# Seven products over the whole depth for the down projections of a hybrid decoder layer

## The chip, the cores and the metric

The kernel runs on one core of one Trainium2 chip. The metric is the device time of one execution in microseconds (us), as the median of several runs on the chip. One execution was also recorded by the hardware profiler; where a text speaks of a place in time, it is the time of that trace, counted from the start of its span.

## What is computed

One decoder layer on 1024 tokens of width 1024, all in float32: a feed-forward network (FFN), a mixer (a gated delta rule beside a Mamba-2 scan), a second FFN, a final RMS norm. The change touches the two FFNs alone, and in them the last product of `swiglu`:

```python
D_MODEL = 1024; SEQ = 1024; D_FF = 2816
def rms_norm(x, w):
    return x * lax.rsqrt(jnp.mean(x * x, axis=-1, keepdims=True) + EPS) * w
def swiglu(h, w_gate, w_up, w_down):
    a = jnp.einsum("bld,df->blf", h, w_gate)
    b = jnp.einsum("bld,df->blf", h, w_up)
    return jnp.einsum("blf,fd->bld", jax.nn.silu(a) * b, w_down)
...
        x = x + 0.5 * swiglu(rms_norm(x, ffn1_norm[i]), ffn1_w_gate[i], ffn1_w_up[i], ffn1_w_down[i])
        x = x + hybrid_mixer(rms_norm(x, mix_norm[i]), ...)
        x = x + 0.5 * swiglu(rms_norm(x, ffn2_norm[i]), ffn2_w_gate[i], ffn2_w_up[i], ffn2_w_down[i])
    return rms_norm(x, final_norm)
```

Below, *hid* is `silu(a) * b`, 1024 tokens by 2816; the down projection is hid times `w_down` (2816 by 1024).

## The kernel before

**Arithmetic.** TensorE works on fp32r data. A float32 operand is split in a high part (a cast, on ScalarE) and a low part (operand minus high part, on VectorE), and each product of two operands is three matmuls: high by high, high by low, low by high (`mm3`, L119 to L121; L311 to L313 in the gate and up phase). One matmul takes 128 of the depth by 128 tokens by 512 columns and adds into a PSUM bank of 128 x 512.

**Stages.** Normalise x and transpose it; gate and up of FFN 1 (`gate_up_all`); its down projection (`down_all`); the mixer; gate and up and down of FFN 2; the final norm. Gate and up already go by Strassen's seven products of 2 x 2 blocks, for 256 columns of hid at a time (pass `p`, 11 of them): the four 512-token quarters `s12, s21, s11, s22` of hid (two column blocks `j` by two token halves) come out of VectorE and are stored in a DRAM scratch, `hid_scr[n][p]` (L390, four stores of 256 KB).

**The down projection before.** `down_all` goes through the depth in 11 groups `g` of 256. For a group, `hid_load` (L401) fetches four pieces of 256 KB from the scratch and splits them, and `load_rows_w` (L152) fetches 1 MB of `w_down` and splits it (`wsplit`, L134 on ScalarE and L135 on VectorE). Then `tile_` is called for 8 token blocks `b` by 2 column halves `dh`: six matmuls into one PSUM bank, and one instruction that adds half of it to the running sum `xt[b]` (VectorE, L420; in group 0, ScalarE writes it, L418). The x of the residual is added piece by piece on the way (L443). The last two groups are taken together, twelve matmuls to a bank, so that a token block is finished as soon as its two banks are: `done(b)` then stores it to `x_scr` and, after blocks 5 and 7, normalises and transposes half of the tokens for the mixer (FFN 1, `norm_mix`), or makes the final norm of the block and stores its output (FFN 2, `finish`, L1209 to L1225). An FFN has 11 x 16 x 6 = 1056 such matmuls in its down projection. All loads and stores named here are issued by SyncE (SP) in program order; a load waits there until its buffer is free, and those behind it in the program wait with it. The order of the instructions on each engine is fixed when the kernel is built.

**Buffers.** `wst` (raw weights) has two buffers, `whi` and `wlo` (split weights) two each; `b0` to `b5` are six buffers in which the gate and up phase keeps operands, and the down projection the split hid. PSUM banks go by tags: `mx` and `sc` two each, `pj` three, `oo` one.

Of the kernel before, what the change touches and what calls it, by code (L numbers as in the profile page):

```python
# [31 lines left out]
NG = GH + SH  # L32
COL_Q, COL_K, COL_V, COL_GZ = 0, 1024, 2048, 3072
# [10 lines left out]
def kernel(  # L44
# [25 lines left out]
    hid_scr = [[dram.tile([P, 2, L], F32, name=f"hid_scr{n}_{i}") for i in range(NF2)] for n in range(2)]  # L70
# [231 lines left out]
    def gate_up_all(pool, H, w_gate, w_up, scr, raws, ops, work, tail):  # L302
# [25 lines left out]
        for i, (p, w) in enumerate(todo):  # L328
# [63 lines left out]
    def hid_load(pool, scr, g):  # L392

        th, tl = (("b0", "b1"), ("b2", "b3"))[g % 2]
        hh = hbp[0].tile([P, 2, L], F32R, name="hid_h", tag=th)
        hl = hbp[0].tile([P, 2, L], F32R, name="hid_l", tag=tl)
        for half in range(2):
            ts = slice(half * 512, (half + 1) * 512)
            for j in range(2):
                t = pool.tile([P, 512], F32, name="hd", tag="q")  # L400
                nc.sync.dma_start(out=t, in_=scr[g][:, j, ts])  # L401
                split(hh[:, j, ts], hl[:, j, ts], t)
        return hh, hl

    def down_all(pool, xt, x_src, w_down, scr, start, before_last, last_tags, done):
        cnt = [0]

        def tile_(tags, b, dh, parts, new=False):
            bs, ds = slice(b * P, (b + 1) * P), slice(dh * 512, (dh + 1) * 512)
            pd = psum(tags[cnt[0] % len(tags)])  # L410
            cnt[0] += 1
            n = 2 * len(parts)
            for i in range(n):
                (hh, hl), (wh, wl) = parts[i // 2]
                j = i % 2
                mm3(pd, hh[:, j, bs], hl[:, j, bs], wh[:, j, ds], wl[:, j, ds], i == 0, i == n - 1)
            if new:
                A.mul(out=xt[b][:, ds], in_=pd, mul=0.5)  # L418
                return
            V.scalar_tensor_tensor(out=xt[b][:, ds], in0=pd, scalar=0.5, in1=xt[b][:, ds],  # L420
                                   op0=ALU.mult, op1=ALU.add)

        nxt = start[0]
        for g in range(NF2 - 2):
            cur = nxt
            hid = hid_load(pool, scr, g + 1)
            if g + 1 < NF2 - 2:
                nxt = hid, load_rows_w(wp, w_down, (g + 1) * 256, "")
            else:
                st = wp.tile([P, 2, D], F32, name="wst", tag="wst")  # L430
                nc.sync.dma_start(out=st, in_=w_down[(g + 1) * 256:(g + 2) * 256].rearrange("(c p) d -> p c d", p=P))
                wh = hbp[0].tile([P, 2, D], F32R, name="whd", tag="b4")
                wl = hbp[0].tile([P, 2, D], F32R, name="wld", tag="b5")
                for j in range(2):
                    split(wh[:, j], wl[:, j], st[:, j])
                nxt = hid, (wh, wl)
            for b in range(NB):
                for dh in range(2):
                    if g == 3 + b // 2:
                        t = pool.tile([P, 512], F32, name="xin", tag="q")  # L440
                        nc.sync.dma_start(out=t, in_=x_src[:, b, dh * 512:(dh + 1) * 512])
                        o = xt[b][:, dh * 512:(dh + 1) * 512]
                        V.tensor_tensor(out=o, in0=o, in1=t, op=ALU.add)  # L443
                    tile_(("mx", "sc", "mx", "sc", "oo"), b, dh, [cur], g == 0)
        last = hid_load(pool, scr, NF2 - 1), load_rows_w(wp, w_down, (NF2 - 1) * 256, "")
        before_last()
        for b in range(NB):
            for dh in range(2):
                tile_(last_tags, b, dh, [nxt, last])
            done(b)  # L450
# [48 lines left out]
    def gate_up_phase(n, npool, H, w_gate, w_up, w_down, raws, ops):  # L499
        start = []  # L500

        def tail_hid():
            start.append([hid_load(npool, hid_scr[n], 0)])

        def tail_w():
            start[0].append(load_rows_w(wp, w_down, 0, ""))

        with tc.tile_pool(name=f"work{n}", bufs=1, side="right", reuse_waits="tile") as work:
            gate_up_all(npool, H, w_gate, w_up, hid_scr[n], raws, ops, work, [tail_hid, tail_w])
        return start  # L510


    with ExitStack() as c1:
# [18 lines left out]
        start = gate_up_phase(0, npool, H, ffn1_w_gate[0], ffn1_w_up[0], ffn1_w_down[0], raws, ops)  # L532
# [719 lines left out]
```

## Time and profile before

| | |
|---|---|
| median of 3 runs | 2404.14 us (2402.14 to 2407.81) |
| profiled execution | 2402.77 us, of which the span of the trace is 2401.1 us |
| TensorE (PE) busy | 2346.9 us, 98% of the span, 12062 matmuls |
| VectorE (DVE) busy | 1680.8 us, 70% |
| ScalarE (ACT) busy | 1042.5 us, 43% |
| DMA | 227.41 MB on SP's queue, packets taking 29.1% of 16 engines' span |
| down projection of FFN 1 | first matmul 462.19 us, last 708.65 us |
| down projection of FFN 2 | first matmul 2150.41 us, last 2391.24 us |

PE's busy time is the time in which matmuls are recorded as running; their ends are modelled, so it says that PE had work, not that it was at its peak. How fast PE goes is read from the distance of one matmul's start to the next.

### The profile page before, as it was taken

How to read it: one execution, taken by the hardware profiler on the slowest of the kernel's cores; microseconds unless marked ns; L12 is line 12 of the kernel's file. 1: busy time of each engine (PE TensorE's matmuls, PEld its weight loads, DVE VectorE, ACT ScalarE, POOL GpSimd, SP SyncE). 2: the span in 40 equal slices, each digit the busy share in tenths (PEclk: the TensorE clock that was granted, in tenths of full speed). 3: DMA queues.
4: the chain of work that ended last, by engine and by line, in shares of the span. 5: the costliest groups of instructions: out<-in, count | busy, mean ns of one | idle time of the engine just before them, and what ended most of it. 6: DMA issues, size and time to landing. Idle time of an engine off the chain costs nothing.

```text
span 2401.1 us, 32017 instructions
## 1 busy us (share of the span) xinstructions
PE 2346.9 (98%) x12062; PEld 1923.1 (80%) x12062; DVE 1680.8 (70%) x3393; ACT 1042.5 (43%) x1972; POOL 52.9 (2%) x117
## 2 busy tenths in 40 slices
PE   6999999999999999999999999999999999999998
PEld 4788888788887878788888888778778888888886
DVE  7766666567756664668777878778686666665777
ACT  7433333422146775863455555412543333343122
POOL 0000000000000010100000000000000000000000
PEclk9999999999999999999999999999999999999999
DMA  2222222433322321222222223235122222242432
GB/s 107 97 81 102 72 88 70 158 105 132 116 106 72 106 88 53 71 91 62 80 80 80 73 78 95 80 121 213 62 88 88 79 80 94 83 151 87 149 106 79
DMA packets 199850, 229.47 MB, mean 96 GB/s; under 512 B 45241, under 2 KB 151926, under 8 KB 198670
## 3 DMA queue, kind: packets, MB, share of 16 engines
q1 hardware_dynamic: 199694, 227.41, 29.1%
q8 instruction: 95, 1.56, 0.3%
q14 instruction: 61, 0.50, 0.1%
HBM read 176.95 MB, written 50.43 MB: 95 GB/s over the span
## 4 chain that ended last, share of the span: by engine, by line
PE 82%; DVE 6%; issue 5%; ACT 4%; DMA 2%; POOL 0%; SPq 0%; DVEq 0%; POOLq 0%; ACTq 0%
PE ps_pj L121 8%; PE ps_pj L119 8%; PE ps_pj L120 8%; PE ps_pj L312 6%; PE ps_pj L311 6%; PE ps_pj L313 6%; PE ps_mx L311 3%; PE ps_mx L312 3%; PE ps_mx L313 3%; PE ps_mx L119 3%; PE ps_mx L121 2%; PE ps_mx L120 2%; PE ps_sc L119 2%; PE ps_sc L121 2%; PE ps_sc L120 2%
## 5 line engine op out<-in xcount | busy, mean ns | idle before, releaser
L119 PE MATMUL ps_pj<-hhi,whi 128*128 128x512 f32 x832 | 334.9, 403 | 0.0
L121 PE MATMUL ps_pj<-hhi,wlo 128*128 128x512 f32 x832 | 332.8, 400 | 0.0
L120 PE MATMUL ps_pj<-hlo,whi 128*128 128x512 f32 x832 | 332.2, 399 | 0.0
L312 PE MATMUL ps_pj<-bl,ah 128*128 128x512 f32 x704 | 274.9, 391 | 1.9 <-DVE bl L217 1.9
L311 PE MATMUL ps_pj<-bh,ah 128*128 128x512 f32 x704 | 274.6, 392 | 1.9 <-ACT sg L371 0.9
L313 PE MATMUL ps_pj<-bh,al 128*128 128x512 f32 x704 | 274.1, 390 | 0.0
L119 PEld LDWEIGHTS ps_pj<-hhi,whi 128*128 128x128 f32 x832 | 156.7, 188 | 28.9 <-issue 0.7
L121 PEld LDWEIGHTS ps_pj<-hhi,wlo 128*128 128x128 f32 x832 | 156.7, 188 | 28.2
L120 PEld LDWEIGHTS ps_pj<-hlo,whi 128*128 128x128 f32 x832 | 156.7, 188 | 27.7
L216 ACT CAST hid_h<-hd 128x512 fp32r<-128x512 f32 x88 | 49.4, 618 | 278.1 <-PE ps_sc L120 117.8
L311 PEld LDWEIGHTS ps_pj<-bh,ah 128*128 128x128 f32 x704 | 131.7, 188 | 32.7 <-ACT bh L216 2.5
L312 PEld LDWEIGHTS ps_pj<-bl,ah 128*128 128x128 f32 x704 | 132.2, 188 | 31.6 <-DVE bl L217 4.7
L313 PEld LDWEIGHTS ps_pj<-bh,al 128*128 128x128 f32 x704 | 132.2, 188 | 27.1
L216 ACT CAST ah<-wst 128x512 fp32r<-128x512 f32 x88 | 54.6, 622 | 218.8 <-PE ps_oo L312 138.9
L290 DVE TENSOR_TENSOR as<-wst 128x512 f32<-128x512 f32 x220 | 142.3, 687 | 1.4 <-DMA wst<-in_ffn_w_up_dram 1.4
L217 DVE TENSOR_TENSOR al<-as,ah 128x512 fp32r<-128x512 f32 x220 | 140.3, 686 | 4.3 <-ACT ah L216 4.3
L311 PE MATMUL ps_mx<-bh,ah 128*128 128x512 f32 x352 | 137.5, 393 | 0.7 <-ACT bh L216 0.4
L312 PE MATMUL ps_mx<-bl,ah 128*128 128x512 f32 x352 | 137.9, 392 | 0.2 <-DVE bl L217 0.2
L313 PE MATMUL ps_mx<-bh,al 128*128 128x512 f32 x352 | 137.7, 391 | 0.0
L135 DVE TENSOR_TENSOR wlo<-wst,whi 128x1024 fp32r<-128x1024 f32 x104 | 125.0, 1222 | 9.6 <-ACT whi L134 8.7
L216 ACT CAST ah<-as 128x512 fp32r<-128x512 f32 x220 | 124.2, 617 | 14.3 <-DVE as L290 14.1
L134 ACT CAST whi<-wst 128x1024 fp32r<-128x1024 f32 x104 | 106.4, 1048 | 44.7 <-PE ps_pj L120 32.4
(398 smaller groups left out, 5093.6 us busy)
## 6 DMA issues: line engine op xcount, KB each, us to landing
wst<-in_ffn_w_gate_dram SPq DMA_DIRECT2D x22, 1024.0 KB, 5.5
wst<-in_ffn_w_up_dram SPq DMA_DIRECT2D x22, 1024.0 KB, 5.0
wst<-in_ffn_w_down_dram SPq DMA_DIRECT2D x22, 1024.0 KB, 5.4
hd<-hid_scr SPq DMA_DIRECT2D x88, 256.0 KB, 3.6
wst<-in_w_in_dram SPq DMA_DIRECT2D x36, 512.0 KB, 5.0
hid_scr<-sg SPq DMA_DIRECT2D x44, 256.0 KB, 2.3
hid_scr<-m SPq DMA_DIRECT2D x42, 256.0 KB, 4.0
wst<-in_w_in_dram SPq DMA_DIRECT2D x8, 1024.0 KB, 4.9
```

The lines of the kernel that those rows point to most:

```text
L119: T.matmul(o, lhsT=wh, rhs=mh, start=first, stop=False)
L120: T.matmul(o, lhsT=wh, rhs=ml, start=False, stop=False)
L121: T.matmul(o, lhsT=wl, rhs=mh, start=False, stop=last)
L134: A.copy(out=hi[sl], in_=st[sl])
L135: V.tensor_tensor(out=lo[sl], in0=st[sl], in1=hi[sl].bitcast(F32), op=ALU.subtract)
L216: A.copy(out=hi, in_=src)
L217: V.tensor_tensor(out=lo, in0=src, in1=hi.bitcast(F32), op=ALU.subtract)
L290: V.tensor_tensor(out=t, in0=v[0], in1=v[1], op=v[2])
L311: T.matmul(bank, lhsT=wh[:, k], rhs=bh[:, k], start=a, stop=False, skip_group_check=True)
L312: T.matmul(bank, lhsT=wh[:, k], rhs=bl[:, k], start=False, stop=False, skip_group_check=True)
L313: T.matmul(bank, lhsT=wl[:, k], rhs=bh[:, k], start=False, stop=z, skip_group_check=True)
```

## The change

The down projection becomes one 2 x 2 Strassen product over the whole depth. hid is cut in two token halves by even and odd 128-row pieces of the depth, `w_down` in the same even and odd pieces by two column halves. Seven products of 512 tokens by 1408 of the depth by 512 columns take the place of eight.

In the gate and up phase, `hid_store` makes, for each pass, five sums or differences of the four quarters (VectorE) and stores seven pieces of 256 KB, one for each product, in place of four. The down projection has 42 steps: the products in the order 3, 2, 5, 4, 1, 7, 6, each in five steps of two 128-row pieces (n = 2) and one of one piece (n = 1). `Down.prep` fetches what a step needs: one or two blocks of `w_down` (products 2 and 5 need one, the others two, 512 KB each at n = 2), the step's hid combination (512 KB), adds the two blocks of weights if there are two, and splits both. Two steps are prepared in the tail of the gate and up phase, and each step prepares the one two ahead. A step is 4 token blocks x n x 3 matmuls into four PSUM banks, which sum the product over its six steps: 132 matmuls a product, 924 an FFN. Products 3 and 5 are summed in the same banks, as are 2 with 4, and 1 with 7. After a product, VectorE (and ScalarE after 3 and 2) carries the four banks into the results that they belong to. x is loaded in eight pieces of 512 KB at the beginning of product 2. After product 7 the first four token blocks are final, and `half_done` normalises them (FFN 1) or finishes them (FFN 2); product 6 completes the other four, its last two steps taken together bank by bank with `done` after each.

```diff
-                for t, j, half in ((s12, 0, 1), (s21, 1, 0), (s11, 0, 0), (s22, 1, 1)):
-                    nc.sync.dma_start(out=scr[p][:, j, half * 512:(half + 1) * 512], in_=t)
+                hid_store(work, scr, p, s11, s21, s12, s22)
+    DOWN_ORDER = (3, 2, 5, 4, 1, 7, 6)
+    BANKS_A, BANKS_B = ("sc", "sc", "mx", "mx"), ("pj", "pj", "pj", "oo")
+    def hid_store(work, scr, p, *blk):
+        for m in DOWN_ORDER:
+            x, *y = HID_OPS[m]
+            t = blk[x]
+            if y:
+                t = work.tile([P, 512], F32, name="hs", tag="hs", bufs=5)
+                V.tensor_tensor(out=t, in0=blk[x], in1=blk[y[0]], op=y[1])
+            i = p - p % 2
+            nc.sync.dma_start(out=scr[m, i][:, p - i], in_=t)
...
+        def prep(self):
...
+            raw = wp.tile([P, 2, 2, 512], F32, name="wst", tag="wst")
+            x, *y = W_OPS[m]
+            for k, blk in enumerate([x] + y[:1]):
+                nc.sync.dma_start(out=raw[:, k, 0:n], in_=self.wv[:, blk // 2, i:i + n,
+                                                                  blk % 2 * 512:(blk % 2 + 1) * 512])
+            src = raw[:, 0, 0:n]
+            hraw = hbp[0].tile([P, 2, 512], F32, name="hraw", tag=f"b{3 + c % 3}")
+            nc.sync.dma_start(out=hraw[:, 0:n], in_=self.scr[m, i])
+            if y:
+                V.tensor_tensor(out=src, in0=src, in1=raw[:, 1, 0:n], op=y[1])
+            w = wp.tile([P, 2, 2, 512], F32R, name="wd", tag=("whi", "wlo")[c % 2])
+            h = hbp[0].tile([P, 2, 2, 512], F32R, name="hid", tag=f"b{c % 3}")
+            split(h[:, 0, 0:n], h[:, 1, 0:n], hraw[:, 0:n])
+            split(w[:, 0, 0:n], w[:, 1, 0:n], src)
...
+            for s, (_, n) in enumerate(DOWN_STEPS):
+                h, w, _ = dn.ready.pop(0)
+                dn.prep()
...
+                for i in range(4):
+                    for h, w, n, z in steps:
+                        product(banks[i], h, w, n, i, m in fresh and z == 0, z == end)
+                    if m == 6 and s == end:
+                        acc(x22[i], banks[i])
+                        done(4 + i)
...
+            elif m == 1:
+                for i in range(4):
+                    acc(x22[i], banks[i])
+            elif m == 7:
+                for i in range(4):
+                    acc(x11[i], banks[i])
+                half_done()
...
+        def norm_first():
+            h2.extend(new_ht())
+            for b in range(4):
+                nc.sync.dma_start(out=x_scr[:, b], in_=xt[b])
+            norm_ht(0, normalise(0, npool, xt), nrm[1], *h2)
...
+    def finish_first():
+        load_wrow()
+        for b in range(4):
+            finish(b)
```

In the changed file the matmuls of `product` are L452 to L454, `acc` is L457, the addition of two weight blocks L435, the split L218 (cast) and L219 (low part), the loads of a step L429 (weights) and L433 (hid). `finish` moves from L1209 to L1225 to L1271 to L1287 without a change.

Three places show how the change moves instructions. The first is SP's queue within the down projection of FFN 1, where the operands are fetched; before (`wst` is a raw weight buffer, `hd` a piece of hid, `xin` of x):

```order
L152 DMA wst<-in_ffn_w_down_dram 128x2x1024
L401 DMA hd<-hid_scr_4_82 128x512 x4
L152 DMA wst<-in_ffn_w_down_dram 128x2x1024
L441 DMA xin<-in_x_dram 128x512 x4
L152 DMA wst<-in_ffn_w_down_dram 128x2x1024
L401 DMA hd<-hid_scr_5_83 128x512 x4
```

and in the change, in the steps of product 4 (`hraw` is a step's hid combination):

```order
L433 DMA hraw<-hid_scr_4_0_96 128x1024
L429 DMA wst<-in_ffn_w_down_dram 128x2x512 x2
L433 DMA hraw<-hid_scr_4_2_97 128x1024
L429 DMA wst<-in_ffn_w_down_dram 128x2x512 x2
L433 DMA hraw<-hid_scr_4_4_98 128x1024
L429 DMA wst<-in_ffn_w_down_dram 128x2x512 x2
L433 DMA hraw<-hid_scr_4_6_99 128x1024
```

A step, which is 24 matmuls, is now fed by two loads of weights and one of hid, 1.5 MB; a group of before, which was 96, by one load of weights and four of hid, 2 MB.

The second is VectorE near the end of FFN 2, where before the banks of the last two groups (`ps_mx`, `ps_sc`) were carried into `xt2b` and a block was finished between them (L114 to L116 and L1216 are steps of its norm, `yo` its output):

```order
L420 SCALAR_TENSOR_TENSOR xt2b<-ps_mx,xt2b 128x512
L116 SCALAR_TENSOR_TENSOR rstd<-rs_t,rstd 128x1
L114 SCALAR_TENSOR_TENSOR rs_t<-rstd,ssv 128x1
L115 TENSOR_TENSOR rs_t<-rs_t,rstd 128x1
L116 SCALAR_TENSOR_TENSOR rstd<-rs_t,rstd 128x1
L1223 SCALAR_TENSOR_TENSOR yo<-xt2b,rstd,wrow 128x512 x2
L420 SCALAR_TENSOR_TENSOR xt2b<-ps_sc,xt2b 128x512
```

In the change, VectorE's rows within product 6 of FFN 2, after the output of block 0 (`wst<-wst` is the addition of weights, `hid` and `wd` the low parts of the last steps):

```order
L1285 SCALAR_TENSOR_TENSOR yo<-xt2b,rstd,wrow 128x512 x2
L435 TENSOR_TENSOR wst<-wst 128x1024
L219 TENSOR_TENSOR hid<-hraw,hid 128x1024
L1278 TENSOR_TENSOR ssv<-ss 128x1
L435 TENSOR_TENSOR wst<-wst 128x512
L1279 TENSOR_SCALAR ssv<-ssv 128x1
L219 TENSOR_TENSOR wd<-wst,wd 128x1024
L112 TENSOR_SCALAR rstd<-ssv 128x1
L219 TENSOR_TENSOR wd<-wst,wd 128x512
```

The finishing of the first four blocks now stands among the preparation of product 6's steps; the outputs of blocks 0, 1 and 2 stand ahead of the first `acc` of product 6, those of 3 to 7 behind it.

The third is PE in FFN 1, where the transposes of the normalised tokens stand among the last matmuls of the down projection. Before, the first of them, after the banks of token block 5:

```order
L121 MATMUL ps_oo<-whi,hid_l 128x512
L194 MATMUL ps_sc<-ident,xtb 128x128 x8
L119 MATMUL ps_mx<-whd,hid_h 128x512
L120 MATMUL ps_mx<-wld,hid_h 128x512
L121 MATMUL ps_mx<-whd,hid_l 128x512
```

and in the change, within product 6:

```order
L454 MATMUL ps_pj<-wd,hid 128x512
L452 MATMUL ps_oo<-wd,hid 128x512
L196 MATMUL ps_sc<-ident,xtb 128x128 x4
L453 MATMUL ps_oo<-wd,hid 128x512
L454 MATMUL ps_oo<-wd,hid 128x512
L452 MATMUL ps_oo<-wd,hid 128x512
L196 MATMUL ps_sc<-ident,xtb 128x128 x4
```

The first four transposes now stand behind 43 matmuls of product 6. The second half's stood behind 28 matmuls of the mixer's first projections and stand behind 23.

More of the change, by code (lines that the diff above doesn't have):

```diff
@@ L32 @@
 NG = GH + SH
+DOWN_STEPS = [(i, min(2, NF2 - i)) for i in range(0, NF2, 2)]
 COL_Q, COL_K, COL_V, COL_GZ = 0, 1024, 2048, 3072
@@ L69 @@
     z_scr = [dram.tile([P, L], F32, name=f"z_scr{i}") for i in range(GH)]
-    hid_scr = [[dram.tile([P, 2, L], F32, name=f"hid_scr{n}_{i}") for i in range(NF2)] for n in range(2)]
+    hid_scr = [{(m, i): dram.tile([P, c, 512], F32, name=f"hid_scr{n}_{m}_{i}")
+                for m in range(1, 8) for i, c in DOWN_STEPS} for n in range(2)]
     g_scr = dram.tile([NG, L], F32, name="g_scr")
@@ new lines, in down_all, with temps, product, acc @@
+    def down_all(pool, xt, x_src, dn, before_last, half_done, done):
+        def temps(name, tags):
+            ts = [ha.tile([P, 2, 512], F32, name=name, tag=tag) for tag in tags]
+            return [ts[i // 2][:, i % 2] for i in range(4)]
+        def product(bank, h, w, n, i, first, last):
+            bs = slice(i * P, (i + 1) * P)
+            for k in range(n):
+                hh, hl, wh, wl = h[:, 0, k, bs], h[:, 1, k, bs], w[:, 0, k], w[:, 1, k]
+                T.matmul(bank, lhsT=hh, rhs=wh, start=first and k == 0, stop=False, skip_group_check=True)
+                T.matmul(bank, lhsT=hh, rhs=wl, start=False, stop=False, skip_group_check=True)
+                T.matmul(bank, lhsT=hl, rhs=wh, start=False, stop=last and k == n - 1, skip_group_check=True)
+        def acc(o, bank, other=None, scale=0.5):
+            V.scalar_tensor_tensor(out=o, in0=bank, scalar=scale, in1=o if other is None else other,
+                                   op0=ALU.mult, op1=ALU.add)
+        def half(ts):
+            return [xt[4 * (ts // 2) + i][:, ts % 2 * 512:(ts % 2 + 1) * 512] for i in range(4)]
+        x11, x12, x21, x22 = (half(ts) for ts in range(4))
+        fresh = {3: "A", 2: "B", 1: "A", 6: "B"}
+        cur = {}
+        end = len(DOWN_STEPS) - 1
+        for m in DOWN_ORDER:
+            if m == 2:
+                for b in range(NB):
+                    nc.sync.dma_start(out=xt[b], in_=x_src[:, b])
+            if m in fresh:
+                cur[fresh[m]] = [psum(t) for t in (BANKS_A if fresh[m] == "A" else BANKS_B)]
+            banks = cur["A" if m in (3, 5, 1, 7) else "B"]
+            steps = []
+            for s, (_, n) in enumerate(DOWN_STEPS):
+                h, w, _ = dn.ready.pop(0)
+                dn.prep()
+                if m == 6 and not dn.todo and before_last:
+                    before_last.pop()()
+                steps.append((h, w, n, s))
+                if m == 6 and s == end - 1:
+                    continue
+                for i in range(4):
[4 more added lines that the diff above has]
+                        done(4 + i)
+                steps = []
+            if m == 3:
+                m3 = temps("m3", ("h0", "h1"))
+                for i in range(4):
+                    A.mul(out=m3[i], in_=banks[i], mul=0.5)
+            elif m == 2:
+                m2 = temps("m2", ("h2", "h3"))
+                for i in range(4):
+                    A.mul(out=m2[i], in_=banks[i], mul=0.5)
+                    V.tensor_tensor(out=m3[i], in0=m3[i], in1=m2[i], op=ALU.subtract)
+            elif m == 5:
+                for i in range(4):
+                    acc(m2[i], banks[i], m3[i], -0.5)
+                    acc(x12[i], banks[i])
+                    V.tensor_tensor(out=x11[i], in0=x11[i], in1=m2[i], op=ALU.add)
+                    V.tensor_tensor(out=x22[i], in0=x22[i], in1=m3[i], op=ALU.add)
+            elif m == 4:
+                for i in range(4):
+                    acc(x11[i], banks[i])
+                    acc(x21[i], banks[i])
+            elif m == 1:
+                for i in range(4):
+                    acc(x22[i], banks[i])
+            elif m == 7:
+                for i in range(4):
+                    acc(x11[i], banks[i])
+                half_done()
@@ L1205, in load_wrow @@
     def load_wrow():
[L1206 removed]
+        wrow.append(ha.tile([P, D], F32, name="wrow", tag="h4"))
         nc.sync.dma_start(out=wrow[0], in_=final_norm.partition_broadcast(P))
```

94 lines of the change are left out of this document (23 added, 71 removed).

## The prediction

> **What bounds the kernel now.** I read the page from the top: busy time by engine, the slices, the chain that ended last.
>
> ```profile
> span 2401.1 us, 32017 instructions
> PE 2346.9 (98%) x12062; PEld 1923.1 (80%) x12062; DVE 1680.8 (70%) x3393; ACT 1042.5 (43%) x1972; POOL 52.9 (2%) x117
> PEclk9999999999999999999999999999999999999999
> PE 82%; DVE 6%; issue 5%; ACT 4%; DMA 2%; POOL 0%; SPq 0%; DVEq 0%; POOLq 0%; ACTq 0%
> ```
>
> PE works through nearly the whole span at its full clock, and 82% of the chain is PE. So a matmul removed is time removed, if the work that feeds it keeps up. How fast PE goes in the down projections is in the table by windows (columns: window, its length, then busy time and instructions of PE, weight loads, DVE, ACT and POOL, granted clock, DMA share, GB/s). The windows are a stretch of the second down projection, the first one whole, gate and up of FFN 1, and a stretch of the mixer:
>
> ```profile
> 2200.00:2300.00 100.00, 99.53 (x440) 82.09 (x439) 79.44 (x119) 18.35 (x26) 0.00 (x0) 1.00 0.43 141
> 462.00:709.00 247.00, 244.28 (x1091) 201.38 (x1090) 162.60 (x245) 65.96 (x100) 0.00 (x0) 1.00 0.36 120
> 70.00:470.00 400.00, 398.22 (x1756) 329.32 (x1755) 266.08 (x424) 146.61 (x258) 0.00 (x0) 1.00 0.28 93
> 1618.00:1624.00 6.00, 6.00 (x31) 4.96 (x31) 4.11 (x7) 0.13 (x1) 0.00 (x0) 1.00 1.01 396
> ```
>
> 440 matmuls in 100 us are 0.2273 us each, without a gap. In the first down projection DVE is busy for 162.60 of 247 us, 66%. What PE waited for there, and in the second, is short (us in total, times, longest):
>
> ```profile
> PE ps_mx L119 <- ACT xtb L418: 2.2, 1, 2.2
> PE ps_sc L119 <- DVE xtb L420: 0.6, 1, 0.6
> PE ps_mx L119 <- ACT xt2b L418: 0.6, 1, 0.6
> PE ps_sc L119 <- DVE xt2b L420: 0.5, 1, 0.5
> ```
>
> These four, 3.9 us, are waits for the first banks to be emptied, at the start of each projection.
>
> **Matmuls removed: -63.9 us.** An FFN loses 1056 - 924 = 132, both lose 264; by 0.2273 that is -60.0 us. The four waits are of L418 and of the second bank's L420, which no longer stand there (the changed product 3 goes through its four banks and keeps them): -3.9. Whether product 3 starts as promptly is in the term of the feed below.
>
> **Work added in gate and up: 0.** Five additions of 128 x 512 a pass. Of this kind the trace has L290, and what such an instruction costs in a queue of others is the distance of their starts:
>
> ```profile
> L290 DVE TENSOR_TENSOR as<-wst x220: 678/687/695, 7.8 to 2128.1; 128x512 f32<-128x512 f32 x110
> 493.25 0.69 DVE L420 SCALAR_TENSOR_TENSOR xtb<-ps_sc,xtb 128x512 f32<-128x512 f32 x1
> 493.85 0.69 DVE L420 SCALAR_TENSOR_TENSOR xtb<-ps_oo,xtb 128x512 f32<-128x512 f32 x1
> ```
>
> So 0.6 us each, 3 us a pass. A pass is some 36 us (400 us for 11), of which DVE works 67% (266.08 of 400); it becomes 75%. Three more stores of 256 KB a pass go to a DMA that is 28% busy there. PE hides both. With no cover it would be 2 x 11 x 3 = 66 us, but nothing else fills a quarter of DVE's time.
>
> **DVE and ACT in the down projection: no term of their own.** A step of two pieces costs DVE up to three instructions of 128 x 1024 (the addition, two low parts), ACT two casts.
>
> ```profile
> L134 ACT CAST whi<-wst x104: 1032/1047/1072, 454.0 to 2329.2; 128x1024 fp32r<-128x1024 f32 x104
> L135 DVE TENSOR_TENSOR wlo<-wst,whi x104: 1212/1222/1229, 455.1 to 2333.8; 128x1024 fp32r<-128x1024 f32 x104
> 490.38 2.36 DVE L135 TENSOR_TENSOR wlo<-wst,whi 128x1024 fp32r<-128x1024 f32 x2
> ```
>
> Two take 2.36 us, so 1.14 in a row: 3.4 us of DVE and 2.1 of ACT in a step's 24 x 0.2273 = 5.46 us of PE. Over an FFN: 30 additions or halves of them, 84 low parts, 40 instructions on banks and x at 0.6, together some 145 us in 210, or 69% against 66% before. DVE keeps up on average; where it is late at one place is priced below.
>
> **The feed: +2 (0 to 8).** This is the step that I am least sure of. A step with two weight blocks brings 1.5 MB in 5.46 us, 288 GB/s, where the window of 2200 to 2300 us moved 141. The rows of the loads now:
>
> ```profile
> wst<-in_ffn_w_down_dram SPq DMA_DIRECT2D x22, 1024.0 KB, 5.4
> wst<-in_w_in_dram SPq DMA_DIRECT2D x36, 512.0 KB, 5.0
> xt<-x_scr SPq DMA_DIRECT2D x8, 512.0 KB
> 1616.07 1.88 SPq L1173 DMA_DIRECT2D xt<-x_scr  x4
> L152 SPq DMA_DIRECT2D wst<-in_ffn_w_down_dram x20: 378/384/384, 425.6 to 2300.1; - x20
> DMA to landing us min/median/max: 4.7/5.4/7.1
> ```
>
> The last two are of the L152 loads of 1 MB (ns of the issue on SP, us to landing). The loop that must hold is that of the two raw weight buffers: issue of two loads (0.4 each), landing (5.4), addition (1.15), cast (1.05), low part (1.22), and the buffer is free: 9.6 us, and up to 1.15 more where hid's low part stands ahead. A buffer serves every second step, and two steps are on average 2 x 132 x 0.2273 / 6 = 10.0 us. It just holds, and a deficit is eaten first from a lead: two steps are prepared ahead, 10.9 us less some 4 to 5 of their splitting, so 6 us. The products with two blocks come as 3, then 2 and 5 with one block, where the lead comes back, then 4, 1, 7, 6: twelve loops on end. At a loop of 10.4 us they lose 12 x 0.4 = 4.8, less than the lead: nothing; at 10.8 it is 9.6 - 6 = 3.6. I take +1 an FFN for single steps late, and 0 to 4 as its ends. While a load of weights waits on SP for its buffer, the hid load behind it waits too; its own buffers are three, so it is not late by that. The x loads at product 2, 4.2 MB or 10.6 us at 396 GB/s, stand ahead of a step's loads; product 2 needs only 1 MB, 2.6 us, a step, so they fit within four steps, and the lead of 6 us covers all but 1 or 2 of it. The bandwidth is there in the row of 1618 to 1624: four loads of 512 KB in a row (1616.07) and 396 GB/s with all 16 engines busy.
>
> By the Trainium skill, page "DMA: Bandwidth & Descriptors", section "Measured (HBM→SBUF, 128 partitions, SWDGE, issued from GpSimd)", DMAs should be batched to 1 MiB or more for 75% of the peak, and the change cuts its weights into 512 KB; section "Terms" has a transfer cost 2.0 us and its bytes over 436e3 a us. By this, an estimate from that page, a load of 512 KB takes 3.2 us, three of them 9.6 us a step if they ran singly, 4.1 more than PE's step, or some 200 us in all. The trace speaks against running singly: 396 GB/s with loads of just that size, issued one behind another; so this is rival 4, with a small chance.
>
> **Bank waits between products 1 and 7: +2.8 (0 to 7).** Products 1 and 7 share banks and follow each other, so PE must wait until DVE has carried bank after bank of product 1, and DVE has the preparation of a step ahead of that in its queue. Bank 0 is ready 3 x 3 x 0.2273 = 2.0 us before the product's end; DVE needs 0.6 for it, and between nothing and a whole preparation (3.4) stands in front. Ends: 0 and 3.4 an FFN; I take 1.4, near the one low part and bank that the order shows there. All other successors have a product between them that covers it.
>
> **First transposes in FFN 1: +1.8 (0 to 3.4).** They stand behind 43 matmuls of product 6, 9.8 us. Their chain: four banks (1.7 us after PE), the square, eleven small ones, two scalings of a block:
>
> ```profile
> 684.09 1.06 ACT L162 ACTIVATE junk<-xtb 128x1024 bf16<-128x1024 f32 x1 [4.29 <-DVE xtb L420]
> 685.27 0.17 DVE L164 TENSOR_SCALAR ssv<-ss 128x4 f32<-128x4 f32 x1 [1.28 <-ACT junk L162]
> 687.73 0.16 DVE L116 SCALAR_TENSOR_TENSOR rstd<-rs_t,rstd 128x4 f32<-128x4 f32 x1
> 687.92 2.19 ACT L184 ACTIVATE xtb<-xtb,rstd 128x1024 f32<-128x1024 f32 x2 [2.69 <-DVE rstd L116]
> ```
>
> From the square's start to the end of the scalings is 684.09 to 690.11, 6.0 us; with 1.7 ahead 7.7, and with one preparation on DVE in between (3.4) 11.1. Against 9.8 that is nothing to +1.3, with ACT's two casts of a step (2.1) up to +3.4; the order sets the small ones among preparations, so I take +1.8. The second half's transposes have five matmuls less before them, 1.1 us; before, they waited 0.27:
>
> ```profile
> 715.72 0.66 PE L194 MATMUL ps_sc<-ident,xn 128*128 128x128 f32 x4 [0.27 <-ACT xn L184]
> ```
>
> No cover is left there, so +1.3 (1 to 2).
>
> **The end of FFN 2: +9.2 (6 to 14).** Before:
>
> ```profile
> 2391.24 0.39 PE L121 MATMUL ps_oo<-whi,hid_l 128*128 128x512 f32 x1
> 2394.40 0.16 DVE L1216 TENSOR_TENSOR ssv<-ss 128x1 f32<-128x1 f32 x1 [0.79 <-ACT junk L1213]
> 2396.53 0.16 DVE L116 SCALAR_TENSOR_TENSOR rstd<-rs_t,rstd 128x1 f32<-128x1 f32 x1
> 2396.72 1.41 DVE L1223 SCALAR_TENSOR_TENSOR yo<-xt2b,rstd,wrow 128x512 f32<-128x512 f32 x2
> ```
>
> From the last matmul's end (2391.5) to the span's is 9.6 us: the bank, the norm, the output (to 2398.1), and 3.0 for its store. A block costs DVE 12 small ones (2394.40 to 2396.72, 2.3 us) and the output, 1.4: 3.7 us. In the change, DVE has from the end of product 7 on: its banks (1.7 left), the preparation of three and a half steps (9 x 1.14 + 3 x 0.6 = 12.1), blocks 0 to 2 (11.1): 24.9 us. Only then comes the first bank of product 6, which PE had ready at (96 + 9) x 0.2273 = 23.9. Then four banks and five blocks, 2.4 + 18.5 = 20.9: DVE ends at 45.8, PE at 30.0, the span 3.0 after DVE. So 18.8 us lie behind the last matmul instead of 9.6: +9.2. It would be 6 if DVE gained on its small instructions, 14 if a late load left it idle once in those 25 us.
>
> **Sum:** -63.9 + 2 + 2.8 + 1.8 + 1.3 + 9.2 = -46.8 against the profiled execution's 2402.77, which is 2356.0; its own time is 1.4 below the median of the runs (2404.14), so I say **2357**. With all the low ends (0, 0, 0, 1, 6) it is 2347, with all the high ones (8, 7, 3.4, 2, 14) 2375.
>
> **Rivals.**
> *1. The feed limits the middle products.* Every pair of weight loads waits behind the 512 KB of hid issued just before it: 1.3 us at 396 GB/s, a loop of 10.4 + 1.3 = 11.7. Twelve loops lose 12 x 1.7 - 6 = 14.4 an FFN, both +29: **2386**. For it: one engine queue and three loads a step. Against: 5.4 us is a landing beside hid loads already.
> *2. The feed makes the kernel slower.* As rival 1, but with the landing at the row's maximum, 7.1: a loop of 13.4. The first three loops lose 10.2 - 6, the twelve 40.8 - 6, together 39 an FFN: +78, **2435**. It decides from a loop of 12.5 us on (51 us lost: the gain is gone, and 0.2% more). Against it: 7.1 is one end of the trace's landings, and 28 to 43% DMA shares leave room.
> *3. DVE is late more often than at the places priced*, as it is in order and two thirds busy: one preparation (3.4 us) late at two more places of each FFN, +14: **2371**.
> *4. Loads run singly*, one landing before the next begins, and the row of a small load gives the price:
>
> ```profile
> hd<-hid_scr SPq DMA_DIRECT2D x88, 256.0 KB, 3.6
> ```
>
> Three loads of at least 3.6 us are 10.8 a step where PE takes 5.46: 5.3 lost in each of the 50 full steps with two blocks: over **2600**. The 396 GB/s above all but exclude it.
> *5. The change doesn't do what it says*: the matmuls that are left are spaced wider, since each bank now gets its six or twelve in turn through six steps; at 0.253 in place of 0.227 the 1848 left take 47 us more, **2404**. Against it: gate and up sum in banks in the same pieces, 1756 in 400 us, 0.228.
>
> **How the numbers follow.** Forecast 0.62; rival 1 0.19; rival 3 0.10; rival 2 0.05; rival 4 0.02; rival 5 0.02. The range 2347 to 2390 holds the forecast's own (2347 to 2375), rival 3 and most of rival 1. A difference of 0.2%, 4.8 us, is about what a measurement of this kernel can tell from none. Faster: the forecast, rivals 1 and 3, 0.91. Same: rival 5, 0.02. Slower: rivals 2 and 4, 0.07.
>
> **What would show it.** PE 11534 matmuls, still 0.227 apart in products; the projections 247 and 241 us long shrink to some 215 and 212; waits of PE on the low part of a step (`wd`) or on `hid` in a few places only; one wait on `acc` between products 1 and 7; some 19 us between the last matmul and the end of the span, DVE without a gap in it. It is wrong if PE waits on L219 or L435 in step after step (the feed: then landings tell which rival), if DVE's share in gate and up rises so that PE waits there, or if the tail is much off 19 us.

## The result and the profile after

| | before | changed |
|---|---|---|
| median | 2403.14 us (4 runs, 2398.6 to 2407.81) | 2365.76 us (4 runs, 2358.4 to 2366.4) |
| ratio, 95% interval | | 0.9837 (0.981 to 0.9865) |
| profiled execution, its span | 2402.77, 2401.1 us | 2366.4, 2364.7 us |

The kernel became 37 us faster where 47 had been forecast; 2365.76 lies in the range of 2347 to 2390. The page of the changed kernel, the lines that answer to those of before:

```profile
PE 2296.1 (97%) x11798; PEld 1880.0 (80%) x11798; DVE 1728.8 (73%) x3359; ACT 1099.4 (46%) x1992; POOL 53.0 (2%) x117
...
PEclk9999999999999999999999999989999999999998
...
PE 72%; DVE 10%; issue 7%; DMA 5%; ACT 4%; POOL 1%; SPq 0%; DVEq 0%; POOLq 0%; ACTq 0%
...
wst<-in_ffn_w_down_dram SPq DMA_DIRECT2D x120, 512.0 KB, 5.4
hraw<-hid_scr SPq DMA_DIRECT2D x70, 512.0 KB, 5.6
```

There are 264 matmuls less, and PE is still the bound, but 28% of the chain is now something else, and the clock row has two slices under full speed. Where the time went is read by stages. The four windows of a kernel are FFN 1's down projection up to the mixer's first matmul, the stages between the projections (mixer, gate and up of FFN 2), FFN 2's down projection, and what lies behind its last matmul. Columns as before: length, busy time and instructions of PE, weight loads, DVE, ACT, POOL, granted clock, DMA share, GB/s. Before:

```profile
462.19:708.87 246.68, 243.96 (x1089) 201.09 (x1088) 162.41 (x245) 65.94 (x100) 0.00 (x0) 1.00 0.36 120
708.87:2150.41 1441.54, 1424.19 (x7973) 1166.07 (x7972) 1026.01 (x2295) 723.96 (x1433) 51.64 (x108) 1.00 0.28 89
2150.41:2391.47 241.06, 239.97 (x1057) 197.86 (x1055) 171.51 (x318) 58.90 (x102) 0.00 (x0) 1.00 0.35 115
2391.47:2401.10 9.63, 0.16 (x1) 0.00 (x0) 5.42 (x18) 0.97 (x4) 0.00 (x0) 0.66 0.28 109
```

The changed kernel:

```profile
462.17:683.78 221.61, 216.20 (x957) 177.32 (x956) 157.22 (x180) 94.60 (x112) 0.00 (x0) 0.99 0.78 271
683.78:2129.91 1446.13, 1428.78 (x7973) 1170.21 (x7972) 1055.65 (x2345) 723.77 (x1430) 51.74 (x108) 0.99 0.30 96
2129.91:2346.28 216.37, 212.02 (x925) 174.14 (x923) 157.02 (x212) 85.25 (x107) 0.00 (x0) 0.99 0.77 268
2346.28:2364.70 18.42, 0.16 (x1) 0.00 (x0) 13.84 (x58) 4.06 (x12) 0.00 (x0) 0.62 0.37 142
```

The two projections gave 25.1 and 24.7 us, not the 29 each of the forecast's terms; the tail grew by 8.8; and 4.6 us went in stages whose code the prediction had at no cost. The first gate and up phase takes as long as before: the projection begins at 462.17 where it began at 462.19, with DVE busier in the window of 70 to 470 us:

```profile
70.00:470.00 400.00, 399.05 (x1761) 330.37 (x1761) 298.50 (x477) 145.68 (x254) 0.00 (x0) 1.00 0.33 115
```

PE's waits in the two changed projections (us in total, times, longest), the first four rows in FFN 1's, the others in FFN 2's:

```profile
PE ps_sc L452 <- DVE xtb L457: 3.0, 1, 3.0
PE ps_sc L196 <- ACT xtb L186: 1.6, 1, 1.6
PE ps_sc L453 <- DVE wd L219: 0.5, 1, 0.5
PE ps_sc L196 <- DVE hlo L214: 0.4, 1, 0.4
...
PE ps_sc L452 <- DVE xt2b L457: 3.1, 1, 3.1
PE ps_pj L452 <- ACT hid L218: 0.9, 1, 0.9
PE ps_sc L453 <- DVE wd L219: 0.3, 1, 0.3
```

The largest is the wait of product 7 for the banks of product 1. DVE's timeline there shows what it had to do first:

```profile
609.48 1.23 DVE L435 TENSOR_TENSOR wst<-wst 128x1024 f32<-128x1024 f32 x1 [2.10 <-DMA wst<-in_ffn_w_down_dram]
611.88 1.23 DVE L219 TENSOR_TENSOR wd<-wst,wd 128x1024 fp32r<-128x1024 f32 x1 [1.17 <-ACT wd L218]
613.02 1.22 DVE L435 TENSOR_TENSOR wst<-wst 128x1024 f32<-128x1024 f32 x1
614.15 1.22 DVE L219 TENSOR_TENSOR hid<-hraw,hid 128x1024 fp32r<-128x1024 f32 x1
615.29 0.68 DVE L457 SCALAR_TENSOR_TENSOR xtb<-ps_sc,xtb 128x512 f32<-128x512 f32 x1
```

The weights land late (2.10 us idle for them), and then three instructions of a preparation, 3.4 us back to back, stand in front of the first bank. PE's first matmul of product 7, in PE's timeline:

```profile
616.12 0.47 PE L452 MATMUL ps_sc<-wd,hid 128*128 128x512 f32 x1 [2.97 <-DVE xtb L457]
```

And the windows around it:

```profile
612.00:616.00 4.00, 1.15 (x6) 0.61 (x4) 4.00 (x5) 2.53 (x3) 0.00 (x0) 1.00 0.49 144
616.00:620.00 4.00, 3.88 (x11) 3.13 (x12) 4.00 (x6) 0.26 (x1) 0.00 (x0) 0.61 0.96 350
620.00:624.00 4.00, 4.00 (x19) 3.25 (x18) 2.40 (x4) 1.07 (x2) 0.00 (x0) 0.96 0.86 258
```

Behind the wait the granted clock is 0.61 over 4 us: 11 matmuls start there where 18 would. In windows of 5 us the loss, (1 - granted clock) x length, adds up to 1.7 us, as much as 3.4 us at half speed. The same is found in FFN 2. So the wait costs 4.7 us in each projection. The loss of any stage is found in the same way: in the stages between the projections it is 5.1 us before and 10.2 after.

### The profile page after: what moved, and what is told of

Read it like the earlier page. It is cut to its first block, busy times and chain, and to the rows that moved or that the text cites. A ratio compares the mean times of both kernels' runs of the same rounds, so it can differ in the third digit from the quotient of the medians.

```text
span 2364.7 us, 31655 instructions
## 1 busy us (share of the span) xinstructions
PE 2296.1 (97%) x11798; PEld 1880.0 (80%) x11798; DVE 1728.8 (73%) x3359; ACT 1099.4 (46%) x1992; POOL 53.0 (2%) x117
## 4 chain that ended last, share of the span: by engine, by line
PE 72%; DVE 10%; issue 7%; DMA 5%; ACT 4%; POOL 1%; SPq 0%; DVEq 0%; POOLq 0%; ACTq 0%
PE ps_pj L121 8%; PE ps_pj L123 8%; PE ps_pj L122 8%; PE ps_pj L314 6%; PE ps_pj L313 6%; PE ps_pj L315 6%; PE ps_mx L313 3%; PE ps_mx L314 3%; PE ps_mx L315 3%; DMA wst<-in_ffn_w_down_dram 3%; PE ps_oo L315 2%; PE ps_oo L313 2%; PE ps_oo L314 2%; DVE hid L219 1%; DMA hraw<-hid_scr 1%
## 5 line engine op out<-in xcount | busy, mean ns | idle before, releaser
L218 ACT CAST ah<-wst 128x512 fp32r<-128x512 f32 x88 | 54.6, 622 | 218.7 <-PE ps_oo L314 139.0
L218 ACT CAST wd<-wst 128x1024 fp32r<-128x1024 f32 x84 | 82.1, 980 | 143.8 <-DVE wst L435 102.1
L219 DVE TENSOR_TENSOR al<-as,ah 128x512 fp32r<-128x512 f32 x220 | 140.2, 685 | 4.3 <-ACT ah L218 4.3
L219 DVE TENSOR_TENSOR wd<-wst,wd 128x1024 fp32r<-128x1024 f32 x84 | 95.0, 1133 | 59.6 <-ACT wd L218 59.2
L218 ACT CAST ah<-as 128x512 fp32r<-128x512 f32 x220 | 124.2, 617 | 14.3 <-DVE as L292 14.1
L218 ACT CAST hid<-hraw 128x1024 fp32r<-128x1024 f32 x84 | 82.2, 980 | 103.1 <-PE ps_mx L454 63.9
```

The source lines that it names most:

```text
L218: A.copy(out=hi, in_=src)
L219: V.tensor_tensor(out=lo, in0=src, in1=hi.bitcast(F32), op=ALU.subtract)
```

## The experiments

Theory A: the missing 10 us are the wait between products 1 and 7, the half clock behind it, and more time at half clock in the mixer; the tail is DVE's queue. The rivals are that DVE or the feed is behind in general, and that the change's own instructions cost the 4.6 us between the projections. All kernels below are the changed one with one edit, if nothing else is said. Lengths of the stages in us, between the same marks as above, and the clock's loss in the stage between:

| kernel | FFN 1 down | between | clock's loss there | FFN 2 down | tail | span | median |
|---|---|---|---|---|---|---|---|
| before | 246.7 | 1441.5 | 5.1 | 241.1 | 9.6 | 2401.1 | 2403.14 |
| changed | 221.6 | 1446.1 | 10.2 | 216.4 | 18.4 | 2364.7 | 2365.76 |
| e1_order | 218.4 | 1450.5 | 10.7 | 212.0 | 21.3 | 2364.8 | 2362.65 |
| e2_finish | 219.7 | 1446.7 | 10.2 | 215.9 | 14.2 | 2358.8 | 2361.40 |
| e3_ffn2_only | 246.9 | 1445.2 | 8.5 | 217.0 | 18.5 | 2389.6 | 2390.43 |
| e4_ffn1_only | 221.9 | 1445.5 | 10.2 | 240.5 | 9.9 | 2380.0 | 2380.57 |
| e5_order_banks | 217.3 | 1441.3 | 3.4 | 210.8 | 21.4 | 2353.0 | 2359.19 |
| e6_all | 217.7 | 1445.1 | 8.5 | 212.7 | 14.2 | 2352.2 | 2353.90 |
| e7_filler | 220.4 | 1442.5 | 3.4 | 215.2 | 19.4 | 2359.8 | 2368.53 |
| e8_feed | 233.0 | 1446.7 | 8.5 | 238.8 | 17.1 | 2398.0 | 2400.76 |
| e9_again | 220.8 | 1440.0 | 3.4 | 216.4 | 18.0 | 2357.4 | 2363.30 |

The stages are those of one profiled execution each. The runs of the changed kernel, e9's with them, lie between 2358.40 and 2368.43 us; of the kernels with both FFNs changed, e6 alone has all its runs below and e8 all its runs above. The other medians don't tell a kernel from the changed one, and what those edits did is read from the stages.

**e1_order: no neighbours on the same banks.**

```diff
-    DOWN_ORDER = (3, 2, 5, 4, 1, 7, 6)
+    DOWN_ORDER = (3, 2, 5, 4, 1, 6, 7)
...
-        x11, x12, x21, x22 = (half(ts) for ts in range(4))
+        x11, x12, x21, x22 = (half(ts) for ts in (3, 2, 1, 0))
```

(and the blocks of `HID_OPS` and `W_OPS` mirrored, 0 with 3 and 1 with 2; the last product is 7.)

> The changed kernel with product 6 set between products 1 and 7, so that no two neighbours share banks (blocks mirrored, so that the first four token blocks are still complete first). Theory A: PE's waits of 3.0 and 3.1 us between products 1 and 7, and the stretch of 3.4 us at half the granted clock behind each (1.7 us lost), come from the shared banks; both go, -9.4 us in all, span about 2355, no granted clock under 1.00 within the down projections. Rival B: DVE is behind by then because the weights land late, and the wait only moves to the start of product 6 or 7 or to the low parts of a step: the waits within the two projections still sum to over 5 us each and the span stays above 2361.

The wait went, and in FFN 2 also the half clock: 216.4 became 212.0, and the projection's clock is 1.00. But the span stayed at 2364.8. In FFN 1 a new wait took the place of the old, 2.3 us at its longest, and 3.4 us of half clock followed it, so the clock there is 0.99 (the row counts from 462 to 700 us):

```profile
PE ps_sc L196 <- DVE hlo L214: 3.2, 4, 2.3
```

The transposes need the `sc` banks, which product 7 now holds to the end; and the tail grew by 2.9, since DVE doesn't end sooner when PE does. The stage between is 4.4 us longer than the changed kernel's, but not all of that is time lost: 12 of the first half's transposes, about 1.1 us by their distances, stand behind the mark here and ahead of it there (945 PE instructions in the projection's window against 957), and 0.5 us is clock. The rest was not taken apart. Theory A was right about the wait between products 1 and 7 and wrong about the span and about FFN 1's clock. The span is where rival B had it, above 2361, but B's cause didn't hold, as the waits on steps stayed at 1.6 us and less in each projection.

**e5_order_banks: the same with the two sets of banks exchanged.**

```diff
-    BANKS_A, BANKS_B = ("sc", "sc", "mx", "mx"), ("pj", "pj", "pj", "oo")
+    BANKS_A, BANKS_B = ("pj", "pj", "pj", "oo"), ("sc", "sc", "mx", "mx")
```

> As e1, with the two sets of banks exchanged (products 3, 5, 1, 7 in the pj and oo banks, 2, 4, 6 in sc and mx). In e1 product 7 held the sc banks that FFN 1's transposes need, and they came late (a wait of 2.3 us, and the stage behind 4.4 us longer than in the changed kernel). Theory: with the sc banks free after product 6 that goes; FFN 1's projection about 216 us (e1 218.4), the stages between the projections back to 1446, FFN 2's projection 212, tail 21: span about 2358. Rival: the transposes are late because the norm's chain is, and FFN 1's projection plus the stages between stay at e1's 1669 us (218.4 + 1450.5).

The projections are 4.3 and 5.6 us shorter than in the changed kernel. The stage between is 1441.3 where 1446 was expected, with a clock's loss of 3.4, and that is nearly all of the 5 us by which the span is below the 2358 expected. FFN 1's projection and the stage behind it are together 10.3 us shorter than in e1, against the rival; but 6.8 of that is clock (12.0 us lost in e1, 5.1 here), and 3.5 is left for the exchange of the banks. FFN 2's projection is 210.8 for 924 x 0.2273 = 210.0 us of matmuls: nothing is left to gain there. The tail is 21.4: 3 of the 5.6 us went straight into it. In FFN 1, 2.4 us of waiting for the norm's chain is left, the forecast's term of +1.8, and half clock behind it (1.7 us lost).

**e2_finish: the final norm in groups.**

```diff
-        for b in range(4):
-            finish(b)
+        finish(0, 4)
...
+    def finish_pair(b):
+        if b % 2:
+            finish(b - 1, 2)
```

(`finish(b0, nb)` works on `[P, nb]` statistics; two outputs a block as before. The square of a block, on ScalarE, is now one instruction of 1024 columns in place of two of 512.)

> The changed kernel with the final norm's small instructions made for four token blocks at once after product 7 and for two at once after product 6 (24 fewer of 128x1 and more in a row removed: 36 for the first four, 24 for the last four). Theory A: the tail of 18.4 us behind the last matmul is DVE's queue (24.9 us of work before the first bank of product 6, then five blocks at 3.7); without it DVE reaches product 6's first bank by 21.8 us, before PE has it, and ends with two blocks: tail about 12 us, -6 us. Rival: the tail is the output's stores and their buffers, and stays above 17 us.

The tail fell from 18.4 to 14.2, with DVE's instructions in it from 58 to 24, and not to 12. In the changed kernel DVE works without a gap from PE's end to its last output, so the tail there is DVE's queue; the rival, the stores, would have kept it above 17. What is left between 14.2 and 12 is seen in e2's trace. DVE's rows of the last bank and of the last pair's norm, with ScalarE's row of the first square between them (`junk`):

```profile
2345.02 0.68 DVE L457 SCALAR_TENSOR_TENSOR xt2b<-ps_oo,xt2b 128x512 f32<-128x512 f32 x1
2348.75 1.06 ACT L1275 ACTIVATE junk<-xt2b 128x1024 bf16<-128x1024 f32 x1 [6.10 <-DMA out_dram<-yo]
2350.97 0.17 DVE L1277 TENSOR_SCALAR ssv<-ss 128x2 f32<-128x2 f32 x1 [2.42 <-ACT junk L1275]
```

`junk` and the outputs `yo` share the buffers of one tag (`q`), so the squares of the last pair wait until a store has left a buffer, and DVE stands idle for 2.42 us. Without that the tail would be 11.8, an estimate from these rows: with DVE's queue shortened, a part of the rival's cause, the stores and their buffers, comes to light. No run gave the squares a buffer of their own.

**e3_ffn2_only and e4_ffn1_only: one FFN changed, the other with the functions of before.**

```diff
+        if n == 0:
+            ...
+            gate_up_all(npool, H, w_gate, w_up, hid_old, raws, ops, work, [tail_hid, tail_w])
+            return start
```

(e4 has `n == 1`; both with `down_all` of before for that FFN.)

> Only FFN 2 has the change; FFN 1's down projection and what follows up to FFN 2's is as before. By stages of the changed trace: FFN 2's projection 241.1 to 216.4 us, its tail 9.6 to 18.4: -15.9 us. Theory A (the 4.5 us that the unchanged stages between the projections lost come with where the clock is lowered behind PE's waits there, not with the change's code in FFN 2): the stages between take 1441.5 us as before and the span is about 2385. Rival: gate and up of FFN 2 with its 55 additions and 33 more stores, or the loads, cost the 4.5: stages between take 1446 us, the span about 2390.

> Only FFN 1 has the change. By stages of the changed trace: FFN 1's projection up to the mixer's first matmul 246.7 to 221.7 us: -25.0; tail and FFN 2's projection as before. Theory A: the mixer's stretches at half clock vary from run to run, so the stages between the projections take 1441 to 1447 us, the span 2376 to 2382; rival: the changed FFN 1 always lengthens them (1446 us, span 2381).

The stages add: -24.1 and +8.8 in the one, -24.8 and +0.2 in the other, within 0.6 us of the changed kernel's. The stages between were longer than before's in both, 1445.2 and 1445.5 us: in e3 that is the rival's length and not theory A's 1441.5, and in e4 both theories allow it. But e4 has no added addition or store in them (DVE's busy time there is before's, 1026 us, against 1056 in the changed kernel), and they are as long as in e3, which has all of them. Both lose more clock there, 8.5 and 10.2 us against 5.1. What settles it is FFN 2's gate and up by itself, where the additions and stores of e3's rival are, from its first matmul to the projection's, before and in the changed kernel:

```profile
1718.91:2150.41 431.50, 429.08 (x1913) 352.55 (x1912) 296.46 (x481) 169.90 (x298) 0.00 (x0) 1.00 0.25 85
1698.43:2129.91 431.48, 429.03 (x1913) 352.54 (x1912) 326.39 (x530) 168.97 (x293) 0.00 (x0) 1.00 0.30 105
```

DVE has 30 us more to do there and the stage takes the same time, so e3's rival is out: the whole 4.6 us lie in the mixer.

**e9_again: the changed kernel once more.**

> The changed kernel once more, unaltered, for the spread and for the stages between the projections. Theory A (what they lost beyond before, 4.6 us, is time at half granted clock behind waits of PE that both kernels have, and it varies from execution to execution): in the profiled execution the stages between take 1441.5 us plus what their granted clock lost beyond the 5.1 us of before, to within 1 us, whatever that loss is; the runs spread over 2358 to 2367 with the mean granted clock going the other way. Rival (the change costs 4.6 us there by its instructions): 1446 us at any loss.

```profile
683.03:2122.99 1439.96, 1422.76 (x7973) 1165.18 (x7972) 1055.71 (x2344) 724.26 (x1430) 51.69 (x108) 1.00 0.30 96
```

With a loss of 3.4 us, 1.7 less than before's, the stages took 1440.0, 1.6 less than before's, as theory A had it. The rival would have 1446. So the 4.6 us of the changed kernel are clock. Less its clock's loss the stage took 1436.4 us before, 1435.9 in the changed kernel and 1436.6 in e9; over the other runs that rest goes from 1435.2 (e4) to 1439.8 (e1), so up to some 3 us of a run's scatter there is not clock, and what it is was not tried. The five runs went from 2358.76 to 2368.43 us, their mean granted clock from 0.993 to 0.991; the ratio was 0.983 (0.9811 to 0.9849). One place shows it: behind the same wait of 1.78 us of the mixer, 17 us of before, of the changed kernel and of e9:

```profile
1563.00:1580.00 17.00, 16.87 (x166) 13.20 (x167) 9.43 (x18) 2.87 (x9) 0.00 (x0) 0.80 0.32 122
1539.00:1556.00 17.00, 16.58 (x146) 12.99 (x147) 8.34 (x15) 2.19 (x6) 0.00 (x0) 0.60 0.33 123
1538.20:1555.20 17.00, 16.57 (x181) 13.07 (x182) 11.49 (x24) 3.39 (x11) 0.00 (x0) 1.00 0.34 124
```

The granted clock is 0.80, 0.60 and 1.00 there: 3.4, 6.8 and 0 us lost with nothing different in that part of the code.

**e7_filler: PE kept busy between products 1 and 7.**

```diff
+            if m == 7:
+                cur["B"] = [psum(t) for t in BANKS_B]
+                for k in range(14):
+                    T.matmul(cur["B"][0], lhsT=h[:, 0, 0, 0:P], rhs=w[:, 0, 0], start=True, stop=True,
+                             skip_group_check=True)
```

> The changed kernel with 14 matmuls of 128x512 added between products 1 and 7 of each FFN, into a bank whose contents product 6 overwrites: PE works through the 3 us in which it otherwise waits for DVE (14 x 0.227 = 3.2 us). The output is not affected. Theory A (the half granted clock behind products 1 and 7 comes from PE having stood idle): the granted clock is 1.00 throughout both projections, each is 1.7 us shorter less 0.2 for the matmuls: 220 and 215 us. Rival (the clock is lowered there for another cause, such as the load of the work since): the stretch at half clock stays, and the projections are as long as in the changed kernel or longer: 221.6 and 216.4.

PE's timeline of the kernel at that place (L478 are the added matmuls), and behind it the windows:

```profile
612.18 3.33 PE L478 MATMUL ps_pj<-wd,hid 128*128 128x512 f32 x14
616.08 0.47 PE L452 MATMUL ps_sc<-wd,hid 128*128 128x512 f32 x1 [0.56 <-DVE xtb L457]
```

```profile
616.00:620.00 4.00, 3.90 (x16) 2.94 (x17) 4.00 (x6) 0.65 (x1) 0.00 (x0) 1.00 0.98 348
620.00:624.00 4.00, 4.00 (x20) 3.30 (x19) 3.08 (x3) 2.11 (x2) 0.00 (x0) 1.00 0.75 264
```

Product 7 starts at the same time, 616.08 against 616.12, DVE and the DMAs do the same, and the clock is 1.00 where it was 0.61. The projections are 220.4 and 215.2, as theory A gave them: the half clock comes from PE's standing idle. That is shown here by stages of the profiled execution; the median of the runs, 2368.53, is not below the changed kernel's, as the stages between scatter by more than these 2.4 us.

**e8_feed: one more load in each step.**

```diff
-            nc.sync.dma_start(out=hraw[:, 0:n], in_=self.scr[m, i])
+            for k in range(2):
+                nc.sync.dma_start(out=hraw2[:, k, 0:n], in_=self.scr[m, i])
```

> The changed kernel with each step's hid loaded twice, the second copy not used: 2 MB in place of 1.5 MB in a step with two weight blocks, 384 GB/s at PE's pace. It prices the feed. Theory (the two raw weight buffers' loop just holds in the changed kernel, and 512 KB more at some 400 GB/s makes it 1.3 us longer, 11 to 11.7 in place of 9.7 to 10.4): twelve loops lose 12 x 1.0 to 1.7, less the lead of 6: 6 to 14 us an FFN, +12 to +29, span 2377 to 2394, with waits of PE on low parts and casts spread over products 4, 1, 7 and 6. Rival (there is much room in the feed): under +5.

The median is 2400.76, ratio 0.9981 (0.9972 to 0.9991) to before: one more load of 512 KB a step takes back nearly all of the gain. The theory's size was low, +35 on the median and +33 on the span for +12 to +29; some 10 us of it are the clock's (5.1 and 8.5 lost in the projections for 1.7 and 1.7). The rows of the loads on its page, and then PE's longest waits in FFN 2, those for the cast of hid:

```profile
hraw<-hid_scr SPq DMA_DIRECT2D x140, 512.0 KB, 7.5
wst<-in_ffn_w_down_dram SPq DMA_DIRECT2D x120, 512.0 KB, 5.7
```

```profile
PE ps_pj L454 <- ACT hid L218: 12.0, 4, 4.9
```

The weights land at 5.7 us, nearly as before; hid, whose row now counts both copies, lands at 7.5 in place of 5.6. But the cast of hid is only the last link. At the longest of these waits, 4.9 us, ScalarE had stood 10.73 us for the weights and then 0.24 us for hid:

```profile
2186.59 1.04 ACT L218 CAST wd<-wst 128x1024 fp32r<-128x1024 f32 x1 [10.73 <-DMA wst<-in_ffn_w_down_dram]
2187.88 1.04 ACT L218 CAST hid<-hraw 128x1024 fp32r<-128x1024 f32 x1 [0.24 <-DMA hraw<-hid_scr]
```

This is in product 2, right behind the eight loads of x, and the DMA is full there, with 410 GB/s:

```profile
2168.00:2188.00 20.00, 16.09 (x70) 12.71 (x69) 5.15 (x5) 6.55 (x10) 0.00 (x0) 1.00 1.03 410
```

FFN 1 has the same wait at the same place, 5.0 us; the other three of FFN 2 are in product 6. What SP stood for before its loads in FFN 2, the changed kernel in two rows and then e8:

```profile
SPq L429 <- DVE wd L219: 55.8, 33, 3.7
SPq L433 <- DVE hid L219: 53.1, 22, 7.3
SPq L429 <- DVE wd L219: 104.7, 33, 9.2
```

A weight buffer is free when its low part is made (`wd`, L219), a hid buffer likewise. With the load added, SP waits for raw weight buffers alone and no longer for hid's. That agrees with the theory's loop of the two weight buffers; its place, "spread over products 4, 1, 7 and 6", was incomplete, as the longest wait is at the x loads.

**e6_all: e5's order and banks with e2's groups.**

> e5's order and banks together with e2's finishing in groups. Theory: the parts add where they lie in different stages: FFN 1's projection 216, stages between 1446, FFN 2's projection 212, and a tail that is shorter than e5's 21 by what e2's was shorter than the changed kernel's (4.2): some 16; span about 2352, median some 2353. Rival: DVE's queue is full over all of the last product, and what PE gains comes back in the tail: 2357 or more.

The median is 2353.90 us (5 runs, 2351.55 to 2357.2), ratio 0.9788 (0.977 to 0.9805): the fastest kernel of the study, 12 us below the changed one, with every run below each of the changed kernel's. The tail is 14.2 with PE's projection at 212.7, so the parts add, and the rival is out. The span is as expected, 2352.2 for 2352, though by other parts than those given: FFN 1's projection and the stages between were 1.7 longer and 0.9 shorter, FFN 2's 0.7 longer, the tail 1.8 shorter.

## Why the prediction was right and where it was not

- **Matmuls, -63.9: right.** 264 less, and e5's 210.8 us for 924 matmuls shows 0.227 each. The count given to look for, 11534, took the 264 off twice; it is 11798.
- **Gate and up, 0: right**, by the start of the first projection (462.17), by FFN 2's gate and up (431.5 us before and after) and by e9.
- **Feed, +2: right**, 0.5 and 1.2 us of waits on steps. The landing that it was worked out with, 5.4 us, is what the changed kernel shows. Rival 1 did not come true, but e8 shows how near it is: 33% more bytes a step, and the gain is gone. The longest wait of e8 is at the x loads of product 2. This step had priced them at the 1 or 2 us that the lead leaves over, and the changed kernel has 0.9 there in FFN 2; with the added load it is 4.9. The formula of 2.0 us and the bytes, cited above rival 4, stands in the Trainium skill, page "DMA: Bandwidth & Descriptors", in the section "Anatomy of one DMA — SWDGE (gpsimd) path", not in "Terms", and is a fit for DMAs issued on that path; the loads here are issued by SyncE.
- **Bank waits, +2.8 (0 to 7): this term failed.** The waits were 3.0 and 3.1 us, and each cost another 1.7 at half clock: 9.5 us together, beyond its upper end. The prediction took "the one low part and bank that the order shows there"; in the trace an addition and two low parts, 3.4 us, stood together in front of the bank, so the upper end of 3.4 an FFN was the one to take. That the weights' late landing pushed them together is argued from the rows and not shown by a run: without the 2.10 us that DVE stood idle, the wait would have been some 0.9 us, an estimate. The half clock behind the wait was in no term. e1 and e5 remove both at this place (in FFN 1 a wait and half clock at the transposes remain), e7 the second alone. Rival 3, DVE late at further places, would have come to nearly the measured time, but the long waits are at the place priced here.
- **First transposes, +1.8, and the second half's, +1.3:** the first is right, 1.6 with 0.4 for a later one; the second was priced too high, 0.46 us of waiting where before had 0.27.
- **The end, +9.2: right**, 8.8. DVE reached product 6's first bank 25.0 us after product 7's end, where 24.9 had been worked out (2341.30, below, and PE's end of 2346.28 less 132 x 0.2273), and PE's end was 18.4 us ahead of the span's. e2 shows that most of it is DVE's. The row of that first bank:

```profile
2341.30 0.69 DVE L457 SCALAR_TENSOR_TENSOR xt2b<-ps_pj,xt2b 128x512 f32<-128x512 f32 x1
```

- **The stages between, 0: not right for this execution**, 4.6 us, by the clock in the mixer. e9 shows it as scatter, so 4.6 us of the miss say nothing about the change.

Summed: the bank waits were 6.7 us dearer than their term and the stages between 4.6, together 11.3; the other terms came out 1.6 cheaper (feed 0.3, transposes 0.9, tail 0.4). That makes 9.7 of the 10.4 us by which the profiled execution (2366.4) exceeded its sum (2356.0). How near the forecast comes also hangs on the execution: e9's, of the same kernel, took 2359.09 us, though its waits between products 1 and 7 were no shorter (3.6 and 3.2 us).

## What to carry to other kernels

When a change makes TensorE's work shorter, look for neighbours that share a bank: a wait there costs its length, and if TensorE stands idle for some 3 us, about half as much again at half clock. What PE gains near the end of the program is worth nothing while the engine behind it has the longer queue; shorten that first (e2), then both add (e6). A feed that shows only 1.7 us of waits can still be one load from its limit, so price it by adding a load before building on it.

## What the runs showed of the hardware

The granted clock falls to a half in pieces of 3.4 us (1.7 us lost, and the stages' losses of 3.4, 5.1, 8.5 and 10.2 us are multiples), mostly after PE has stood idle. All eight waits of 3.0 to 4.5 us between products 1 and 7 in the changed kernel, e2, e3, e4 and e9 were followed by it or had it begin within them, and so was a wait of 4.2 us in the mixer in every trace. Of waits of 2.2 to 2.8 at the transposes of e1, e5, e6 and e7, two of four were: 2.30 and 2.36 us, but not 2.2 and 2.82. So e6's unbroken clock in FFN 1, beside e5's loss, is luck. A wait of 1.78 among small matmuls of the mixer was followed sometimes by none, sometimes by 6.8 us lost. And in five traces, the changed kernel's among them, a piece of half clock stands at 866 us (within 2 us), where no wait is longer than 0.3 us and 16 matmuls of 128x2 have just run; e5 has the same rows without it. So idle time that shows as a wait is not the whole of it. The Trainium skill, page "TensorE: Matmul & The Clock Gate", section "What's actually happening", has the clock halved after an idle window of about 3.4 us, and back after a busy one of that length; the length and the half agree with these traces, but waits of 3.0 us and less were enough here. Runs of one kernel differ by up to 10 us, most of it with the clock: of the changed kernel, three runs of 2365.72 to 2366.4 us had a mean granted clock of 0.991, the one of 2358.4 had 0.994, and 0.003 x 2364 = 7 us is their distance. What decides which of these waits is followed by half clock was not tried.
